# Opening of a hybrid decoder layer: the weight casts are queued behind the cast of h, and the low gate weights ride beside the high ones

## The chip, the core and the metric

The kernel runs on one core of a Trainium2 chip. The metric is the device time of one execution in microseconds. A kernel's time is the median of its runs; beside that there is one profiled execution, from which all rows below come. The engines are called as the profile calls them: PE (TensorE, matrix products), PEld (its weight loads), DVE (VectorE), ACT (ScalarE), POOL (GpSimd) and SP (SyncE, which here only issues transfers).

## What is computed

The reference is one decoder layer over 512 tokens of width 2048, in 32-bit floats. The opening, with which this case deals, computes `h` and the first columns of `h @ w_in`:

```
mod = jax.nn.silu(c) @ w_ada + b_ada
shift, scale, gate = jnp.split(mod[:, None, :], 3, axis=-1)
h = rms_norm(x, norm_w) * (1.0 + scale) + shift
proj = h @ w_in
aq, ak, av, ag, d_qkv, dz, db, da, mg_a, mg_b = jnp.split(proj, _split_points(), axis=-1)
...
beta = jax.nn.sigmoid(db.astype(f32))
g = -jnp.exp(a_log) * jax.nn.softplus(da.astype(f32) + dt_bias)
```

The rest (sliding-window attention, the gated delta rule, the merge and the output product) is the same in both kernels.

## The kernel before

Each product of 32-bit operands is made of three products of a shorter format. An operand is split into a high part, the cast of the value, and a low part, the value less the high part. `mm3` then adds up high weights times high `h`, high weights times low `h`, and low weights times high `h`. `split` makes the two parts: the cast on ACT (line 61, tile `whi`), the subtraction on DVE (line 62, tile `wlo`). For `h` the two parts are `hh` (ACT, line 476) and `hl` (DVE, line 480).

`startup` is the opening. The width of 2048 is cut into 16 blocks of 128 rows, numbered `kt` from 0 to 15. For each block the kernel needs the shift and the scale of these 128 rows. They are sums of `silu(c)` over two tiles of `w_ada` of 1 MB each (tile `wa`, lines 394 and 458). In blocks with an even number, and in block 15, one of the two sums is made on PE (line 449, picked up on line 455), the other on DVE; in the other blocks both are made on DVE. In block 0 both are made on PE. From the sums ACT makes the shift and scale (lines 468 and 471, tile `sh`), then `h` of the block (line 475), then `hh`; DVE makes `hl`. With these `products` runs 21 products of 512 columns: seven column groups of weights (two for `v`, one of 64 columns called `ba` for the gates' `db` and `da`, four for `k`), three products each.

The weights of these column groups come as one tile of 832 KB for two blocks (tile `raw`, line 215, source `w_st`). `split_half` splits the half that belongs to one block, 832 columns. `whl` keeps three pairs of high and low tiles, `wraw` two raw tiles, `st2` seven `wa` tiles. `half_done` puts the next split on a list, and `weight_tick` runs the list at the end of a block.

The order in which the instructions stand on each engine is made by a scheduler from the program; each engine then works through its own row in order. `behind(a, b)` tells the scheduler that `a` must stand after `b`. `split_behind` is used for this in the opening: the subtraction of the weights of block `kt + 1` is put behind the last DVE sum of `wa` for that block (`last_sum`). The cast of these weights has no such rule in the kernel before. `made["h"]` holds the latest cast of `h`; when the split of the weights of block `kt + 1` is put out, it is the cast of `h` of that same block.

After the opening, `gates` takes the 64 rows of `ba`, turns them with four transposes (line 566) and makes the gates of them.

Of the kernel before, what the change touches and what calls it, by code (L numbers as in the profile page):

```python
# [7 lines left out]
F32 = mybir.dt.float32  # L8
# [3 lines left out]
ALU = mybir.AluOpType  # L12
# [4 lines left out]
P = 128  # L17
T = 512
D = 2048
KT = D // P  # L20
NTB = T // P
EPS = 1e-6
KH = 16
VH = 32
# [7 lines left out]
NST = 4  # L32
# [13 lines left out]
class Layer:  # L46
# [174 lines left out]
    def split_half(self):  # L221
        n = self.half_split
        j = n // 2
        if j < len(self.jobs):
            w = self.jobs[j][1].shape[-1] // 2
            raw = self.raws[j]
            hi = self.whl.tile([P, 1024], F32R, tag="whi", name="whi")
            lo = self.whl.tile([P, 1024], F32R, tag="wlo", name="wlo")
            h, l = self.split(hi[:, :w], lo[:, :w], raw[:, (n % 2) * w : (n % 2 + 1) * w])
            if self.split_behind:  # L230
                self.behind(l, self.split_behind)
            self.halves[n] = (hi, lo)
            self.half_split += 1
            if n % 2:
                del self.raws[j]
                self.due.append(self.load_job)
# [144 lines left out]
    def startup(self, st):  # L381


        tc, nc, a, const = self.tc, self.nc, self.a, self.const
# [3 lines left out]
        acc, loads, sums, made = {}, {}, {}, {}  # L388
        last_sum = {}

        def load_ada(kt):
# [13 lines left out]
            out=row, in0=scb[0:1, :], scalar=1.0, in1=row, op0=ALU.add, op1=ALU.mult  # L405
# [23 lines left out]
        for g in range(4):  # L429
# [3 lines left out]
            out=bn, in0=self.b_ada[:, KT : 2 * KT], scalar=1.0, in1=self.norm_w, op0=ALU.add, op1=ALU.mult  # L433
# [52 lines left out]
        n = 0  # L486
        for q in range(4):
            ps = self.psc.tile([P, T], F32, tag="sc", name="rowb")
# [5 lines left out]
        for b2 in (0, 2):  # L494
# [3 lines left out]
            for b in (b2, b2 + 1):  # L498
                xt, u = xts[b], b % 2
                nc.vector.tensor_scalar(out=xt, in0=xt, scalar1=r[:, u : u + 1], scalar2=None, op0=ALU.mult)  # L500
                for q in range(4):
                    i = n % 6
                    ps = pa.tile([P, 4, P], F32, tag=f"x{i}", name="xtp") if i < 2 else self.psc.tile([P, 4, P], F32, tag="sc", name="xtp")
# [11 lines left out]
        def products(kt, parts):  # L515
            f, l = kt == 0, kt == KT - 1
            wh, wl = parts
            x = (self.hh[:, kt, :], self.hl[:, kt, :])
            for ps, o, n in outs:
                self.mm3(ps, (wh[:, o : o + n], wl[:, o : o + n]), x, f, l)  # L520

        low(0, adaln(0))
        ada_sums(1)
        acc_v = [pa.tile([P, T], F32, tag=f"x{i}", name=f"v{i}") for i in range(2)]
        acc_ba = self.pmm.tile([P, T], F32, tag="mm", name="ba")[: 2 * VH]
        self.acc_k = [self.psc.tile([P, T], F32, tag="sc", name=f"k{n}") for n in range(NST)]
        outs = [(acc_v[0], 0, P), (acc_v[1], P, P), (acc_ba, 2 * P, 2 * VH)]
        outs += [(self.acc_k[n], 320 + n * P, P) for n in range(NST)]
        for kt in range(KT):
            nxt = kt + 1 < KT and adaln(kt + 1)  # L530
            if kt + 3 < KT:
                load_ada(kt + 3)
            if kt + 2 < KT:
                ada_sums(kt + 2)
            if kt + 1 < KT:
                low(kt + 1, nxt)
            products(kt, self.half(f"st{kt // 2}"))
            self.half_done()
            self.split_behind = last_sum.get(kt + 1)
            self.weight_tick()  # L540
        self.split_behind = None
        self.ba = self.dnc.tile([2 * VH, T], F32, name="ba")
        nc.vector.tensor_copy(out=self.ba, in_=acc_ba)
        for i in range(2):
            vt = s2.tile([P, T], F32, tag="h32", name="vt")
# [5 lines left out]
    def gates(self, sp):  # L551

        nc, a, dnc = self.nc, self.a, self.dnc
        pt = self.ptp
        bd = sp.tile([P, NTB, 2 * VH], F32, name="bd")
        S = [P, NTB, VH]
        self.sums = sp.tile([P, 4, P], F32, name="sums")
        nc.sync.dma_start(out=self.sums, in_=a["k_sums"])
        al = sp.tile([P, VH], F32, name="al")
        nc.sync.dma_start(out=al, in_=a["a_log"].partition_broadcast(P))  # L560
        dtb = sp.tile([P, VH], F32, name="dtb")
        nc.sync.dma_start(out=dtb, in_=a["dt_bias"].partition_broadcast(P))
        nc.scalar.activation(al, al, AF.Exp)
        pb = pt.tile([P, NTB, 2 * VH], F32, tag="tp", name="pb")
        for c in range(NTB):
            nc.tensor.transpose(pb[:, c, :], self.ba[:, c * P : (c + 1) * P], self.ident[: 2 * VH, : 2 * VH])
        nc.vector.tensor_copy(out=bd, in_=pb)
        beta = self.beta = dnc.tile(S, F32, name="beta")
        e = sp.tile(S, F32, name="ge")
        nc.scalar.activation(e, bd[:, :, 0:VH], AF.Exp, scale=-1.0)  # L570
        nc.vector.tensor_scalar(out=e, in0=e, scalar1=1.0, scalar2=None, op0=ALU.add)
        nc.vector.reciprocal(out=beta, in_=e)
        y = sp.tile(S, F32, name="gy")
        nc.vector.tensor_tensor(out=y, in0=bd[:, :, VH : 2 * VH], in1=dtb.unsqueeze(1).to_broadcast(S), op=ALU.add)
        u = sp.tile(S, F32, name="gu")
        nc.vector.scalar_tensor_tensor(out=u, in0=y, scalar=-1.0, in1=y, op0=ALU.mult, op1=ALU.min)
        nc.scalar.activation(u, u, AF.Exp)
        w = sp.tile(S, F32, name="gw")
        nc.vector.tensor_scalar(out=w, in0=u, scalar1=1.0, scalar2=None, op0=ALU.add)
        lw = sp.tile(S, F32, name="glw")  # L580
        nc.scalar.activation(lw, w, AF.Ln)
        d = sp.tile(S, F32, name="gd")
        nc.vector.scalar_tensor_tensor(out=d, in0=w, scalar=-1.0, in1=u, op0=ALU.add, op1=ALU.subtract)
        nc.vector.reciprocal(out=w, in_=w)
        nc.vector.tensor_tensor(out=d, in0=d, in1=w, op=ALU.mult)
        nc.vector.tensor_tensor(out=lw, in0=lw, in1=d, op=ALU.subtract)
        nc.vector.scalar_tensor_tensor(out=y, in0=y, scalar=0.0, in1=lw, op0=ALU.max, op1=ALU.add)
        nc.vector.scalar_tensor_tensor(
            out=y, in0=y, scalar=-1.0, in1=al.unsqueeze(1).to_broadcast(S), op0=ALU.mult, op1=ALU.mult
        )  # L590
        fl = lambda t: t.rearrange("p c h -> p (c h)")
        yield 8
        pg = pt.tile([P, 4, P], F32, tag="tp", name="pg")
        for n in range(4):
            nc.tensor.matmul(pg[:, n, :], lhsT=self.sums[:, n, :], rhs=fl(y), start=True, stop=True)
        G = sp.tile(S, F32, name="G")
        nc.vector.tensor_copy(out=fl(G), in_=pg[:, 0, :])
        EG = sp.tile(S, F32, name="EG")
        nc.scalar.activation(fl(EG), pg[:, 1, :], AF.Exp)
        self.kd = dnc.tile(S, F32, name="kd")  # L600
        nc.scalar.activation(fl(self.kd), pg[:, 2, :], AF.Exp)
        self.egl = dnc.tile(S, F32, name="egl")
        nc.scalar.activation(fl(self.egl), pg[:, 3, :], AF.Exp)
        self.neg_eg = dnc.tile(S, F32, name="neg_eg")
        nc.vector.tensor_scalar(out=self.neg_eg, in0=EG, scalar1=-1.0, scalar2=None, op0=ALU.mult)
        self.neg_g = dnc.tile(S, F32, name="neg_g")
        nc.vector.tensor_scalar(out=self.neg_g, in0=G, scalar1=-1.0, scalar2=None, op0=ALU.mult)
        self.neg_beta = dnc.tile(S, F32, name="neg_beta")
        nc.vector.tensor_scalar(out=self.neg_beta, in0=beta, scalar1=-1.0, scalar2=None, op0=ALU.mult)
        self.g_rows = self.dram.tile([VH, T], F32, name="g_rows")  # L610
        self.eg_rows = self.dram.tile([VH, T], F32, name="eg_rows")
        self.b_rows = self.dram.tile([VH, T], F32, name="b_rows")
        for src, dst in ((G, self.g_rows), (EG, self.eg_rows), (beta, self.b_rows)):
            yield 1
            pr = pt.tile([VH, T], F32, tag="tp", name="pr")
            for c in range(NTB):
                nc.tensor.transpose(pr[:, c * P : (c + 1) * P], src[:, c, :], self.ident)
            rows = sp.tile([VH, T], F32, tag="rows", name="rows", bufs=2)
            nc.vector.tensor_copy(out=rows, in_=pr)
            nc.sync.dma_start(out=dst, in_=rows)  # L620
        self.dump("G", G)
        self.dump("beta", beta)
# [1063 lines left out]
def layout(i):  # L1686
# [3 lines left out]
    f = lambda x: np.ascontiguousarray(x)  # L1690
    w_in, w_ada = i["w_in"][0], i["w_ada"][0]
    o = {}
# [9 lines left out]
    o["b_ada"] = f(i["b_ada"][0].reshape(48, P).T)  # L1702
    o["b_gate"] = f(i["b_ada"][0].reshape(3, D)[2])
    o["norm_w"] = f(i["norm_w"][0].reshape(KT, P).T)
    st = np.concatenate([w_in[:, 2304:2560], w_in[:, 16896:16960], w_in[:, 6656 : 6656 + NST * P]], 1)
    o["w_st"] = f(st.reshape(KT // 2, 2, P, STW).transpose(0, 2, 1, 3).reshape(KT // 2, P, 2 * STW))
    ch = lambda w: w.reshape(KT, P, -1, P).transpose(2, 1, 0, 3).reshape(-1, P, KT * P)
    o["w_ch"] = f(np.concatenate([ch(w_in[:, 4608:16896]), ch(w_in[:, 19008:]), ch(w_in[:, :2304]), ch(w_in[:, 2560:4608]), ch(w_in[:, 16960:19008])]))
# [57 lines left out]
```

## Time and profile before

| | before |
|---|---|
| median of 3 runs | 2849.0 us (2845.32 to 2851.39) |
| time of the profiled execution | 2842.31 us |
| its span, first to last instruction | 2840.5 us |
| granted TensorE clock over the span | 0.999 |
| PE busy in the span | 2812.2 us (99%) |
| DVE, ACT busy | 1940.2 us (68%), 1195.2 us (42%) |
| products of blocks 0 to 15 in the opening | from 31.08 us to 124.86 us |

In the rows of a timeline the first number is the start in us, the second the busy time in us, then come engine, line, operation, output and inputs; the brackets tell how long the engine was idle before, and what ended that. A row of the windows gives for a stretch the busy time of each engine with the count of its instructions, then the granted PE clock, the share of the transfer engines that was busy, and GB/s. Consecutive starts on an engine are closer than the durations, since instructions overlap a little; the sums below go from start to start.

### The profile page before, as it was taken

To read this page: it belongs to the slowest core of one execution; us is meant where nothing else is said; L and a number is where in the kernel's file an instruction comes from. 1 tells how busy PE (TensorE), PEld (TensorE's weight loads), DVE (VectorE), ACT (ScalarE), POOL (GpSimd) and SP (SyncE) were. 2 spreads that over 40 slices of the span, in tenths; PEclk is the share of its full clock that TensorE was granted. 3 is DMA by queue.
4 is the path that set the end of the run, shared out by engine and by line. 5 is a ranking of instruction groups with operands and counts; after the bars stand their busy time and mean duration, and the time that the engine had idled before them with its cause. 6 is when DMAs were issued, how large, how long until landed. Compare 5 with 4: busy or idle time off the path is not lost.

```text
span 2840.5 us, 38583 instructions
## 1 busy us (share of the span) xinstructions
PE 2812.2 (99%) x14312; PEld 2305.0 (81%) x14312; DVE 1940.2 (68%) x3142; ACT 1195.2 (42%) x2452; POOL 146.9 (5%) x124
## 2 busy tenths in 40 slices
PE   8999999999999999999999999999999999999999
PEld 5788888887787888888888888888888888888887
DVE  7866776867757666778766666666656766664676
ACT  5555443244454343433434333333334554432443
POOL 0010100100000010000001000000000000000000
PEclk9999999999999999999999999999999999999999
DMA  9878764322244253366777666666646887885684
GB/s 404 333 230 238 255 223 143 110 91 92 80 118 137 87 167 105 116 209 218 243 259 262 231 223 241 230 231 235 242 167 233 300 311 246 303 276 179 245 312 172
DMA packets 228368, 603.30 MB, mean 212 GB/s; under 512 B 76210, under 2 KB 102450, under 8 KB 187858
## 3 DMA queue, kind: packets, MB, share of 16 engines
q1 hardware_dynamic: 228180, 600.83, 62.2%
q8 instruction: 113, 1.85, 0.3%
q14 instruction: 75, 0.61, 0.1%
HBM read 480.35 MB, written 118.17 MB: 211 GB/s over the span
## 4 chain that ended last, share of the span: by engine, by line
PE 94%; DVE 2%; DMA 2%; ACT 1%; issue 1%; SPq 0%; POOL 0%; DVEq 0%; ACTq 0%; POOLq 0%
PE mm L259 22%; PE mm L261 21%; PE mm L260 21%; PE m L260 5%; PE m L259 5%; PE m L261 5%; PE S L1416 1%; PE pv L960 1%; PE O L1474 1%; PE pod L979 1%; PE pod L978 1%; PE pod L975 1%; PE pp L950 1%; DMA E<-g_rows 1%; PE k L259 1%; PE k L260 1%
## 5 line engine op out<-in xcount | busy, mean ns | idle before, releaser
L259 PE MATMUL mm<-hh,whi 128*128 128x512 f32 x2784 | 1129.1, 406 | 0.0
L261 PE MATMUL mm<-hh,wlo 128*128 128x512 f32 x2784 | 1089.2, 391 | 0.0
L260 PE MATMUL mm<-hl,whi 128*128 128x512 f32 x2784 | 1086.4, 390 | 0.0
L62 DVE TENSOR_TENSOR wlo<-raw,whi 128x1024 fp32r<-128x1024 f32 (+1 forms) x532 | 653.2, 1228 | 438.1 <-ACT whi L61 432.4
L61 ACT CAST whi<-raw 128x1024 fp32r<-128x1024 f32 (+1 forms) x532 | 555.9, 1045 | 838.3 <-PE mm L260 595.5
L261 PEld LDWEIGHTS mm<-hh,wlo 128*128 128x128 f32 x2784 | 522.5, 188 | 113.8 <-issue 0.4
L259 PEld LDWEIGHTS mm<-hh,whi 128*128 128x128 f32 x2784 | 523.4, 188 | 111.7 <-issue 10.6
L260 PEld LDWEIGHTS mm<-hl,whi 128*128 128x128 f32 x2784 | 524.0, 188 | 100.8 <-issue 1.6
L1225 DVE TENSOR_TENSOR q<-q,q 128x1024 f32<-128x1024 f32 x96 | 124.8, 1300 | 0.7 <-issue 0.6
L773 ACT ACTIVATE E<-E,neg_g 128x128 f32<-128x128 f32 x256 | 80.9, 394 | 90.5 <-POOL E L767 78.9
L810 DVE TENSOR_TENSOR A<-A,atmp 128x62 f32<-128x62 f32 (+30 forms) x124 | 109.2, 881 | 0.4
L802 DVE TENSOR_TENSOR atmp<-A 128x62 f32<-128x62 f32 (+30 forms) x124 | 107.4, 866 | 0.3
L907 POOL TENSOR_TENSOR qe<-qe,yq 128x512 f32<-128x512 f32 x32 | 55.6, 1755 | 920.1 <-DMA qe<-eg_rows 532.2
L980 ACT COPY osb<-pod 128x256 f32<-128x256 f32 x64 | 23.8, 372 | 152.6 <-PE pod L979 152.6
L767 POOL TENSOR_SCALAR_AFFINE_SELECT E<-E 128x512 f32<-128x512 f32 x64 | 59.3, 941 | 433.2 <-DMA E<-g_rows 241.5
L962 ACT COPY vn<-pv 128x256 f32<-128x256 f32 x64 | 23.8, 372 | 124.4 <-PE pv L960 124.4
L631 DVE SCALAR_TENSOR_TENSOR yv<-mm,convh,yv 128x511 f32<-128x511 f32 (+2 forms) x96 | 71.2, 742 | 1.1
L967 DVE TENSOR_SCALAR vs<-vn,kd 128x128 f32<-128x128 f32 x96 | 23.1, 283 | 58.3 <-ACT vn L962 58.3
L1444 ACT ACTIVATE sm<-sm,mx,rs 128x128 f32<-128x128 f32 x128 | 61.5, 482 | 3.0 <-DVE mx L1439 3.0
L990 DVE SCALAR_TENSOR_TENSOR S<-S,egl,pod 128x128 f32<-128x128 f32 x64 | 19.2, 342 | 51.0 <-ACT junk L983 51.0
L636 ACT ACTIVATE th<-yv 128x512 f32<-128x512 f32 x32 | 20.2, 631 | 76.3 <-DVE yv L631 73.7
L458 DVE SCALAR_TENSOR_TENSOR wa<-wa,silu_cb 128x2048 f32<-128x2048 f32 x22 | 50.1, 2283 | 0.0
(438 smaller groups left out, 3661.4 us busy)
## 6 DMA issues: line engine op xcount, KB each, us to landing
raw<-in_w_ch SPq DMA_DIRECT2D x158, 1024.0 KB
wa<-in_w_ada_ss SPq DMA_DIRECT2D x32, 1024.0 KB
q<-in_w_od SPq DMA_DIRECT2D x64, 512.0 KB
g_d<-q SPq DMA_DIRECT2D x64, 512.0 KB
raw<-g_d SPq DMA_DIRECT2D x32, 1024.0 KB
raw<-in_w_od SPq DMA_DIRECT2D x24, 1024.0 KB
gw<-in_w_ada_gate SPq DMA_DIRECT2D x16, 1024.0 KB
E<-g_rows SPq DMA_DIRECT2D x64, 256.0 KB
```

What stands on the lines that cost most here:

```text
L61: h = self.nc.scalar.copy(out=hi, in_=src)
L62: l = self.nc.vector.tensor_tensor(out=lo, in0=src, in1=hi.bitcast(F32), op=ALU.subtract)
L259: nc.tensor.matmul(ps, lhsT=wh, rhs=xh, start=first, stop=False)
L260: nc.tensor.matmul(ps, lhsT=wh, rhs=xl, start=False, stop=False)
L261: self.last_mm = nc.tensor.matmul(ps, lhsT=wl, rhs=xh, start=False, stop=last)
L631: nc.vector.scalar_tensor_tensor(out=y[:, s:], in0=ps[:, : T - s], scalar=w[:, j : j + 1], in1=y[:, s:], op0=ALU.mult, op1=ALU.add)
L767: self.last_mask = self.nc.gpsimd.affine_select(out=E, in_=E, pattern=[[0, NTB], [1, P]], compare_op=ALU.is_ge, fill=NEG, base=0, channel_ ...
L773: self.nc.scalar.activation(E[:, c, :], E[:, c, :], AF.Exp, bias=self.neg_g[:, c, h : h + 1])
L802: eng.tensor_tensor(out=t, in0=A[:, m : m + 1, m + 1 :].to_broadcast([P, m, n]), in1=A[:, :m, m : m + 1].to_broadcast([P, m, n]), op=ALU.mult,
L810: self.behind(eng.tensor_tensor(out=A[:, :m, m + 1 :], in0=A[:, :m, m + 1 :], in1=t, op=ALU.add))
L1225: self.behind(nc.vector.tensor_tensor(out=q[f], in0=q[x], in1=q[y], op=ALU.add))
L1444: nc.scalar.activation(t, t, AF.Exp, scale=r[:, h : h + 1], bias=mx[:, h : h + 1], accum_out=den[:, h : h + 1])
```

## The change

There are two edits, both in the opening.

The first edit is in `split_half`. `split_behind` is now a pair. The cast of the weights (now line 231) is put behind the cast of `h` of the same block, `made["h"]`. The subtraction stays behind the last DVE sum.

The second edit concerns the 64 gate columns. They move to the end of the 832 columns. Their low part is no longer written into `wlo` but into `whi`, right behind the high part, so that high and low stand side by side in 128 columns. One product of these 128 columns with `hh` then takes the place of two of 64 columns. High times high lands in rows 0 to 63 of `ba`, low times high in rows 64 to 127; the product with `hl` is still of 64 columns. A block has 20 products instead of 21. The subtraction of one half becomes two instructions (both line 232): 768 columns into `wlo` and 64 into `whi`. In `gates` the four transposes take 128 rows, and one more addition joins the two halves.

```diff
             hi = self.whl.tile([P, 1024], F32R, tag="whi", name="whi")
             lo = self.whl.tile([P, 1024], F32R, tag="wlo", name="wlo")
-            h, l = self.split(hi[:, :w], lo[:, :w], raw[:, (n % 2) * w : (n % 2 + 1) * w])
+            src = raw[:, (n % 2) * w : (n % 2 + 1) * w]
+            if w < 1024:
+                h = self.nc.scalar.copy(out=hi[:, :w], in_=src)
+                sub = lambda out, s: self.nc.vector.tensor_tensor(
+                    out=out, in0=src[:, s], in1=hi[:, s].bitcast(F32), op=ALU.subtract
+                )
+                wide, ba = slice(0, 6 * P), slice(6 * P, w)
+                l = sub(lo[:, wide], wide)
+                low = (l, sub(hi[:, w : w + 2 * VH], ba))
+            else:
+                h, l = self.split(hi[:, :w], lo[:, :w], src)
+                low = (l,)
             if self.split_behind:
-                self.behind(l, self.split_behind)
+                self.behind(h, self.split_behind[0])
+                for i in low if self.split_behind[1] else ():
+                    self.behind(i, self.split_behind[1])
...
-            for ps, o, n in outs:
+            for i, (ps, o, n) in enumerate(outs):
+                if i == 2:
+                    pair = [(P, x[0]), (2 * VH, x[1])]
+                    for m, xm in pair[::-1] if l else pair:
+                        nc.tensor.matmul(
+                            acc_ba[:m], lhsT=wh[:, 6 * P : 6 * P + m], rhs=xm, start=f and m == P, stop=l and m == P
+                        )
                 self.mm3(ps, (wh[:, o : o + n], wl[:, o : o + n]), x, f, l)
...
-        outs = [(acc_v[0], 0, P), (acc_v[1], P, P), (acc_ba, 2 * P, 2 * VH)]
-        outs += [(self.acc_k[n], 320 + n * P, P) for n in range(NST)]
+        outs = [(acc_v[0], 0, P), (acc_v[1], P, P)]
+        outs += [(self.acc_k[n], 2 * P + n * P, P) for n in range(NST)]
...
-            self.split_behind = last_sum.get(kt + 1)
+            self.split_behind = (made["h"], last_sum.get(kt + 1))
...
-        self.ba = self.dnc.tile([2 * VH, T], F32, name="ba")
+        self.ba = self.dnc.tile([P, T], F32, name="ba")
...
-        pb = pt.tile([P, NTB, 2 * VH], F32, tag="tp", name="pb")
+        pb = pt.tile([P, NTB, P], F32, tag="tp", name="pb")
         for c in range(NTB):
-            nc.tensor.transpose(pb[:, c, :], self.ba[:, c * P : (c + 1) * P], self.ident[: 2 * VH, : 2 * VH])
-        nc.vector.tensor_copy(out=bd, in_=pb)
+            nc.tensor.transpose(pb[:, c, :], self.ba[:, c * P : (c + 1) * P], self.ident)
+        nc.vector.tensor_copy(out=bd, in_=pb[:, :, 0 : 2 * VH])
+        nc.vector.tensor_tensor(out=bd, in0=pb[:, :, 2 * VH :], in1=bd, op=ALU.add)
```

What the edits do to the order is seen best on ACT, from the shift and scale of block 4 to the cast of `h` of block 5. `whi_554` and `whi_611` are the high weights of blocks 4 and 5, `h32_520` and `h32_561` their `h` (one number higher after the change), `acc` the sums of DVE. Before:

```order
L471 ACTIVATE sh_517<-acc_470,bn_154,norm_wT_114 128x1
L61 CAST whi_554<-raw_454 128x832
L475 ACTIVATE h32_520<-xnT_94,sh_517 128x512
L61 CAST whi_611<-raw_454 128x832
L476 CAST hh_76<-h32_520 128x512
L468 ACTIVATE sh_558<-acc_527,b_adaT_112 128x1
L471 ACTIVATE sh_558<-acc_527,bn_154,norm_wT_114 128x1
L475 ACTIVATE h32_561<-xnT_94,sh_558 128x512
L476 CAST hh_76<-h32_561 128x512
```

The same stretch of ACT's row after the change:

```order
L484 ACTIVATE sh_518<-acc_471,bn_154,norm_wT_114 128x1
L488 ACTIVATE h32_521<-xnT_94,sh_518 128x512
L489 CAST hh_76<-h32_521 128x512
L231 CAST whi_554<-raw_454 128x832
L481 ACTIVATE sh_559<-acc_528,b_adaT_112 128x1
L484 ACTIVATE sh_559<-acc_528,bn_154,norm_wT_114 128x1
L488 ACTIVATE h32_562<-xnT_94,sh_559 128x512
L489 CAST hh_76<-h32_562 128x512
L231 CAST whi_611<-raw_454 128x832
```

Both casts stood ahead of the `hh` of block 4; now each stands right behind the `hh` of its own block, and `whi_611` has moved past the four instructions of block 5.

On DVE, the stretch from the sum of block 4 to the first sum of block 7 stands so before:

```order
L458 SCALAR_TENSOR_TENSOR wa_427,acc_470<-wa_427,silu_cb_93 128x2048
L62 TENSOR_TENSOR wlo_555<-raw_454,whi_554 128x832
L458 SCALAR_TENSOR_TENSOR wa_466,acc_527<-wa_466,silu_cb_93 128x2048
L480 TENSOR_TENSOR hl_77<-h32_520,hh_76 128x512
L458 SCALAR_TENSOR_TENSOR wa_468,acc_527<-wa_468,silu_cb_93 128x2048
L62 TENSOR_TENSOR wlo_612<-raw_454,whi_611 128x832
L458 SCALAR_TENSOR_TENSOR wa_525,acc_568<-wa_525,silu_cb_93 128x2048
L480 TENSOR_TENSOR hl_77<-h32_561,hh_76 128x512
L62 TENSOR_TENSOR wlo_653<-raw_552,whi_652 128x832
L458 SCALAR_TENSOR_TENSOR wa_564,acc_625<-wa_564,silu_cb_93 128x2048
```

DVE after the change, from the same sum on:

```order
L471 SCALAR_TENSOR_TENSOR wa_428,acc_471<-wa_428,silu_cb_93 128x2048
L232 TENSOR_TENSOR wlo_555<-raw_454,whi_554 128x768
L471 SCALAR_TENSOR_TENSOR wa_467,acc_528<-wa_467,silu_cb_93 128x2048
L493 TENSOR_TENSOR hl_77<-h32_521,hh_76 128x512
L232 TENSOR_TENSOR whi_554<-raw_454,whi_554 128x64
L471 SCALAR_TENSOR_TENSOR wa_469,acc_528<-wa_469,silu_cb_93 128x2048
L232 TENSOR_TENSOR wlo_612<-raw_454,whi_611 128x768
L232 TENSOR_TENSOR whi_611<-raw_454,whi_611 128x64
L471 SCALAR_TENSOR_TENSOR wa_526,acc_569<-wa_526,silu_cb_93 128x2048
L493 TENSOR_TENSOR hl_77<-h32_562,hh_76 128x512
L232 TENSOR_TENSOR wlo_653<-raw_552,whi_652 128x768
L471 SCALAR_TENSOR_TENSOR wa_565,acc_626<-wa_565,silu_cb_93 128x2048
```

Sums and subtractions keep their places; the 64-column subtractions are new, one behind the wide one in an odd block, one behind `hl` in an even block.

On PE, block 14 after the change begins so; the transposed sum of block 15 (line 462) stands ahead of it:

```order
L462 MATMUL ada<-wa,silu_cr 32x128 x16
L272 MATMUL v_351<-hh,whi 128x512
L272 MATMUL v_352<-hh,whi 128x512
L468 MATMUL ada<-pick,adas 128x1
L536 MATMUL ba<-hh,whi 128x512
L272 MATMUL k_354<-hh,whi 128x512
L272 MATMUL k_355<-hh,whi 128x512
L272 MATMUL k_356<-hh,whi 128x512
L272 MATMUL k_357<-hh,whi 128x512
L273 MATMUL v_351<-hl,whi 128x512
L274 MATMUL v_351<-hh,wlo 128x512
```

And before:

```order
L449 MATMUL ada<-wa,silu_cr 32x128 x16
L261 MATMUL k_357<-hh,wlo 128x512
L259 MATMUL v_351<-hh,whi 128x512
L455 MATMUL ada<-pick,adas 128x1
L259 MATMUL v_352<-hh,whi 128x512
L259 MATMUL ba<-hh,whi 64x512
L259 MATMUL k_354<-hh,whi 128x512
L259 MATMUL k_355<-hh,whi 128x512
L259 MATMUL k_356<-hh,whi 128x512
L259 MATMUL k_357<-hh,whi 128x512
L260 MATMUL v_351<-hl,whi 128x512
```

In both, the seven products that need only `hh` and `whi` come first, and the products with `hl` and `wlo` after them; the product of the gate columns with `hh` now has 128 rows of output.

More of the change, by code (lines that the diff above doesn't have):

```diff
@@ L524, in startup @@
         acc_v = [pa.tile([P, T], F32, tag=f"x{i}", name=f"v{i}") for i in range(2)]
-        acc_ba = self.pmm.tile([P, T], F32, tag="mm", name="ba")[: 2 * VH]
+        acc_ba = self.pmm.tile([P, T], F32, tag="mm", name="ba")
         self.acc_k = [self.psc.tile([P, T], F32, tag="sc", name=f"k{n}") for n in range(NST)]
-        outs = [(acc_v[0], 0, P), (acc_v[1], P, P), (acc_ba, 2 * P, 2 * VH)]
-        outs += [(self.acc_k[n], 320 + n * P, P) for n in range(NST)]
+        outs = [(acc_v[0], 0, P), (acc_v[1], P, P)]
+        outs += [(self.acc_k[n], 2 * P + n * P, P) for n in range(NST)]
         for kt in range(KT):
@@ L1704, in layout @@
     o["norm_w"] = f(i["norm_w"][0].reshape(KT, P).T)
-    st = np.concatenate([w_in[:, 2304:2560], w_in[:, 16896:16960], w_in[:, 6656 : 6656 + NST * P]], 1)
+    st = np.concatenate([w_in[:, 2304:2560], w_in[:, 6656 : 6656 + NST * P], w_in[:, 16896:16960]], 1)
     o["w_st"] = f(st.reshape(KT // 2, 2, P, STW).transpose(0, 2, 1, 3).reshape(KT // 2, P, 2 * STW))
```

## The prediction

> **What bounds the opening now.** I read the page first, then the windows of the opening, then the timeline of PE, DVE and ACT there.
>
> ```profile
> PE 2812.2 (99%) x14312; PEld 2305.0 (81%) x14312; DVE 1940.2 (68%) x3142; ACT 1195.2 (42%) x2452; POOL 146.9 (5%) x124
> 97.50:108.50 11.00, 11.00 (x88) 8.45 (x76) 9.78 (x11) 5.72 (x11) 0.00 (x0) 1.00 1.01 420
> ```
>
> PE is busy 99% of the span, so nothing outside the opening can give back much of what the opening loses. In the window PE is full, DVE is busy 9.78 of 11 us, and the transfers run at 420 GB/s. PE sets the pace, but DVE is only 1.2 us behind it.
>
> ```profile
> 53.14 0.73 PE L259 MATMUL v<-hh,whi 128*128 128x512 f32 x2
> ...
> 97.68 0.73 PE L259 MATMUL v<-hh,whi 128*128 128x512 f32 x2
> ...
> 108.70 0.73 PE L259 MATMUL v<-hh,whi 128*128 128x512 f32 x2
> ...
> 120.06 0.39 PE L259 MATMUL v<-hh,whi 128*128 128x512 f32 x1
> ...
> 124.86 0.39 PE L259 MATMUL mm<-hh,whi 128*128 128x512 f32 x1
> ```
>
> These are the first products of blocks 3, 11, 13 and 15, and the first after the opening. Two blocks take 108.70 - 97.68 = 11.02 us. The 21 products of block 15 take 4.80 us, 0.2286 each. So 42 products are 9.60 us of the pair's 11.02, and 1.42 us go to the sum on PE.
>
> DVE and ACT in such a pair:
>
> ```profile
> 88.89 1.02 DVE L62 TENSOR_TENSOR wlo<-raw,whi 128x832 fp32r<-128x832 f32 x1 [1.22 <-ACT whi L61]
> 89.83 2.28 DVE L458 SCALAR_TENSOR_TENSOR wa<-wa,silu_cb 128x2048 f32<-128x2048 f32 x1
> ...
> 92.04 0.69 DVE L480 TENSOR_TENSOR hl<-h,hh 128x512 fp32r<-128x512 f32 x1
> 92.64 2.28 DVE L458 SCALAR_TENSOR_TENSOR wa<-wa,silu_cb 128x2048 f32<-128x2048 f32 x1
> ...
> 94.86 1.02 DVE L62 TENSOR_TENSOR wlo<-raw,whi 128x832 fp32r<-128x832 f32 x1
> 95.79 2.28 DVE L458 SCALAR_TENSOR_TENSOR wa<-wa,silu_cb 128x2048 f32<-128x2048 f32 x1
> ```
>
> ```profile
> 87.98 0.87 ACT L61 CAST whi<-raw 128x832 fp32r<-128x832 f32 x1
> 88.76 0.81 ACT L475 ACTIVATE h<-xnT,sh 128x512 f32<-128x512 f32 x1
> 89.48 0.87 ACT L61 CAST whi<-raw 128x832 fp32r<-128x832 f32 x1
> 90.25 0.62 ACT L476 CAST hh<-h 128x512 fp32r<-128x512 f32 x1
> ...
> 94.97 0.39 ACT L471 ACTIVATE sh<-acc,bn,norm_wT 128x1 f32<-128x1 f32 x1 [2.52 <-DVE wa L458]
> 95.39 0.82 ACT L475 ACTIVATE h<-xnT,sh 128x512 f32<-128x512 f32 x1
> 96.24 0.62 ACT L476 CAST hh<-h 128x512 fp32r<-128x512 f32 x1
> ```
>
> One of the two `wlo` of a pair, at 88.89, waits 1.22 us for its cast; the other, at 94.86, starts at once, because its cast was done at 89.48, before the sums ahead of it.
>
> **The first edit, on the steady pairs.** After the change every `wlo` stands on DVE right behind the last sum of its own block (in even blocks `hl` of the block before stands between), while its cast stands on ACT behind that block's `sh`, `h` and `hh`, which need this very sum. So from the start of the last sum to the start of `wlo` there is one chain: sum to `sh` 94.97 - 92.64 = 2.33; `sh` to `h` 0.42; `h` to `hh` 0.85; `hh` to the next ACT instruction 0.53; the cast 0.87; cast's end to `wlo` 88.89 - 88.85 = 0.04. The 0.53 is from these rows:
>
> ```profile
> 39.59 0.62 ACT L476 CAST hh<-h 128x512 fp32r<-128x512 f32 x1
> 40.12 0.26 ACT L454 COPY adas<-ada 128x128 f32<-128x128 f32 x1
> ```
>
> The chain is 5.04 us. DVE has nothing else to do in it beyond the sum (2.21 from start to start) and, in even blocks, `hl` (0.60): what is behind `wlo` in its row, the next block's sums, waits too, and with them ACT and PE.
>
> From start to start on DVE: `wlo` of 832 columns 89.83 - 88.89 = 0.94, of 768 columns 0.94 x 768/832 = 0.87 (an estimate by width). No row has a subtraction of 64 columns. The nearest small ones are these:
>
> ```profile
> 142.05 0.22 DVE L605 TENSOR_SCALAR neg_eg<-EG 128x128 f32<-128x128 f32 x1
> 142.18 0.22 DVE L607 TENSOR_SCALAR neg_g<-G 128x128 f32<-128x128 f32 x1
> ```
>
> They are 0.13 apart and 0.22 long, which are my bounds; I take 0.14, since 64 columns are fewer than 128 and read two inputs.
>
> - From `wlo` of an odd block to `wlo` of the even one: 0.87 + 0.14 + 5.04 = 6.05 us.
> - From there to the next odd one: 0.87 + a first sum 2.21 + `hl` 0.60 + 0.14 + 5.04 = 8.86 us.
> - A pair: 14.91 us, where PE alone took 11.02. That is 3.89 us more per pair, and DVE becomes the bound, by waiting 2.83 + 2.23 = 5.06 us per pair instead of 1.22.
>
> **The start.** Here the edit gains.
>
> ```profile
> 27.64 0.89 ACT L61 CAST whi<-raw 128x832 fp32r<-128x832 f32 x1
> ...
> 28.90 0.84 ACT L475 ACTIVATE h<-xnT,sh 128x512 f32<-128x512 f32 x1
> ...
> 30.39 0.63 ACT L476 CAST hh<-h 128x512 fp32r<-128x512 f32 x1
> ...
> 37.35 0.89 ACT L61 CAST whi<-raw 128x832 fp32r<-128x832 f32 x1 [5.55 <-PE k L260]
> ```
>
> ```profile
> 33.87 2.29 DVE L458 SCALAR_TENSOR_TENSOR wa<-wa,silu_cb 128x2048 f32<-128x2048 f32 x1
> 40.26 0.51 PE L259 MATMUL v<-hh,whi 128*128 128x512 f32 x1 [1.71 <-ACT hh L476]
> ```
>
> A cast between `h` and `hh` of block 0 goes away: `hh` starts at 28.90 + 0.85 = 29.75 instead of 30.39, 0.64 sooner. The cast at 37.35 waited for a tile that PE held until the end of block 0, and block 1's `sh` stood behind it; that wait goes. So the last sum of block 1 starts at 33.87 - 0.64 = 33.23, and its `wlo` and PE's block 1 at 33.23 + 5.04 = 38.27 instead of 40.26: 2.0 us gained. Block 2: 38.27 + 6.05 = 44.32. Its `hl` starts 0.82 before that (0.04 + 0.87 + 0.53, less 0.62 for `hh`) at 43.50; then `hl` 0.60, a sum 2.21, `wlo` 0.87 lead to 47.18, and the chain of 5.04 to `wlo` of block 3 at 52.22, against 53.14 for PE's block 3 before. What is gained is 0.9 us.
>
> **The rest.** Five pairs lead to block 13 at 52.22 + 74.55 = 126.77, then 14 at 132.82 and 15 at 138.87 (both with one DVE sum, 6.05 each). In block 14 PE does the seven `hh` products and waits for `hl`, which stands behind the sum of block 15: 132.82 + 0.87 + 0.14 + 2.21 + 0.69 = 136.73. From there PE has 13 + 20 products without a wait: 33 x 0.2286 = 7.54, ending at 144.27. Before, it was 124.86. The opening gets 19.4 us longer.
>
> **The second edit.** It removes 16 products, 16 x 0.2286 = 3.66 us of PE. PE waits for DVE in every pair (14.91 against 40 x 0.2286 + 1.42 = 10.56), so I count 0 for it, besides the one product already left out in block 14 and in block 15. It would count in full only with PE as the bound. The 16 small subtractions are in the chain above, 0.14 each.
>
> ```profile
> 126.31 0.46 PE L566 MATMUL pb<-ident,ba 64*128 64x64 f32 x4
> 127.53 0.42 DVE L567 COPY bd<-pb 128x256 f32<-128x256 f32 x1
> ```
>
> In `gates` the transposes may take up to twice their 0.46 us on PE and the addition costs another 0.42 on DVE; between 0 and 0.9 us, and I take 0, since the gates had until 134 us to wait for other loads. The weight load of 128 columns instead of 64 hides beside the product, as for `v` and `k`.
>
> **Loads** do not become the bound.
>
> ```profile
> wa<-in_w_ada_ss SPq DMA_DIRECT2D x32, 1024.0 KB
> raw<-in_w_st SPq DMA_DIRECT2D x8, 832.0 KB
> ```
>
> A pair needs four `wa` and one `raw`, 4928 KB or 5.05 MB, 12.0 us at 420 GB/s. SP issues a `raw` only when the odd block's subtraction has read the old one, and the `wa` loads queue behind it; at 14.91 us a pair there are 2.9 us to spare.
>
> **Sum.** 2842.3 + 19.4 = 2861.7 us for the profiled execution, which was 6.7 us under the median of the runs. Against the median, 2849.0 + 19.4 = 2868.4.
>
> **Rivals.**
>
> *PE goes cold in its new idle stretches, and the loss is larger.* Each pair has about 3.3 us of waits inside its blocks (some 1.9 for `hl` in the odd, 1.4 in the even).
>
> ```profile
> 37.50:40.90 3.40, 1.68 (x36) 1.32 (x35) 0.66 (x2) 2.81 (x6) 0.00 (x0) 1.00 1.01 424
> 40.90:44.30 3.40, 3.31 (x8) 2.31 (x9) 3.40 (x6) 1.35 (x3) 0.00 (x0) 0.50 1.00 417
> 208.20:211.60 3.40, 1.57 (x11) 1.49 (x12) 2.94 (x11) 2.73 (x7) 0.00 (x0) 1.00 0.23 81
> 211.60:215.00 3.40, 3.40 (x19) 2.81 (x18) 1.77 (x3) 1.52 (x6) 0.00 (x0) 1.00 0.82 163
> ```
>
> Once 3.4 us with PE busy for 1.68 were followed by a window at half clock, once with 1.57 they were not. A cold window costs 1.7 us of PE work. Two per pair with all waits kept give 10.56 + 3.4 + 3.3 = 17.3 us, 2.4 over DVE's 14.91; over six pairs 14 us more, 2883. Against it: a late PE finds `hl` ready and has no idle stretch left, so the loss grows only up to the waits. It decides when a pair of PE passes 14.91. [...]
>
> *DVE does not hold PE up, and the edits pay.* It would need the casts early enough that each `wlo` waits no more than the present 1.22 us per pair. Then PE stays the bound, with 3.66 us of products less and the 2.0 us at block 1: 2849.0 - 5.7 = 2843.3, on the edge of what can be told from no change (0.2%, 5.7 us, is about what the measurement tells). For it speaks only the gain at the start; against it, that the sum, `sh`, `h`, `hh`, cast and `wlo` depend on each other in this order. It decides where the chain shrinks from 5.04 to about 3.1 us.
>
> *The order does less than it says*, because some `wlo` finds its cast done, as at 94.86 now. If this held for one block of each pair, 2.83 us of the wait would go: 14.91 - 2.83 = 12.08, 1.06 over 11.02. Six pairs make 6.4, less the 0.9 gained at the start 5.5, so 2849.0 + 5.5 = 2854.5. The row on ACT gives no block such a cast.
>
> **Chances.** 0.80 for the forecast, 0.09 for the cold PE, 0.05 for edits that pay, 0.06 for the partial case. The forecast's own range: small subtractions at 0.22 add 1.2 us, `gates` up to 0.9, one cold window in blocks 14 and 15 1.7; hand-overs 0.05 off in each of 15 blocks 0.8 either way; the median of the runs moves some 3 us. That is 2862 to 2876. For eight in ten I give 2860 to 2878. Faster by over 0.2%: 0.02; within 0.2%: 0.08 (half of the partial case with it); slower: 0.90.
>
> **What would show it.** After the change, each `wlo` on DVE waits for ACT's `whi`: about 2.8 us in odd and 2.2 us in even blocks, over 30 us in all. Wide subtractions two blocks apart are 14.9 us apart. PE's block 1 starts near 38.3, block 15 near 139, the first product after the opening near 144. PE has idle stretches with `hl` and `whi` as releasers, DVE busy falls to two thirds in a pair's window, and the transfers fall under 420 GB/s. From 150 us on both kernels should run alike, shifted. The forecast is wrong if `wlo` finds its cast done, or if the granted clock is 0.50 in many windows of the opening.

## The result and the profile after

The changed kernel takes 2870.98 us (median of 4 runs, 2865.76 to 2874.23) against 2847.16 us before (4 runs, 2843.12 to 2851.39): a ratio of 1.0081 with an interval of 1.0066 to 1.0095, slower by 24 us. Its profiled execution took 2874.23 us with a span of 2872.5 us. All rows of "the changed kernel" below are of this execution.

From its page, the engines' busy time and the chain that ended last:

```profile
PE 2818.7 (98%) x14296; PEld 2308.0 (80%) x14296; DVE 1939.4 (68%) x3159; ACT 1196.4 (42%) x2452; POOL 148.4 (5%) x124
...
PE 88%; DVE 5%; DMA 3%; ACT 3%; issue 1%; SPq 0%; POOL 0%; DVEq 0%; ACTq 0%; POOLq 0%
```

And the chain on the page of the kernel before:

```profile
PE 94%; DVE 2%; DMA 2%; ACT 1%; issue 1%; SPq 0%; POOL 0%; DVEq 0%; ACTq 0%; POOLq 0%
```

The 16 products are gone from PE (14296 against 14312), yet PE's share of the chain has fallen by 6 points, and DVE and ACT have taken over most of it. The view by windows says where. This is one pair of blocks of the changed kernel, from the wide subtraction of block 9 to that of block 11:

```profile
97.67:112.57 14.90, 11.21 (x74) 8.26 (x74) 10.02 (x12) 5.93 (x12) 0.00 (x0) 1.00 0.84 340
```

Before, a pair took 11.02 us with PE full. Now PE is busy 11.21 of 14.90 us, DVE 10.02 and ACT 5.93, and the transfers have fallen from 420 to 340 GB/s. No engine and no queue is full, which is what a chain of hand-overs looks like. The timeline of DVE in the pair before it, and of ACT at its end:

```profile
82.76 0.96 DVE L232 TENSOR_TENSOR wlo<-raw,whi 128x768 fp32r<-128x768 f32 x1 [2.74 <-ACT whi L231]
83.63 0.22 DVE L232 TENSOR_TENSOR whi<-raw,whi 128x64 fp32r<-128x64 f32 x1
83.77 2.29 DVE L471 SCALAR_TENSOR_TENSOR wa<-wa,silu_cb 128x2048 f32<-128x2048 f32 x1
...
88.81 0.96 DVE L232 TENSOR_TENSOR wlo<-raw,whi 128x768 fp32r<-128x768 f32 x1 [2.14 <-ACT whi L231]
89.69 2.28 DVE L471 SCALAR_TENSOR_TENSOR wa<-wa,silu_cb 128x2048 f32<-128x2048 f32 x1
...
91.90 0.69 DVE L493 TENSOR_TENSOR hl<-h,hh 128x512 fp32r<-128x512 f32 x1
92.50 0.22 DVE L232 TENSOR_TENSOR whi<-raw,whi 128x64 fp32r<-128x64 f32 x1
92.64 2.28 DVE L471 SCALAR_TENSOR_TENSOR wa<-wa,silu_cb 128x2048 f32<-128x2048 f32 x1
...
97.67 0.96 DVE L232 TENSOR_TENSOR wlo<-raw,whi 128x768 fp32r<-128x768 f32 x1 [2.74 <-ACT whi L231]
```

```profile
94.97 0.39 ACT L484 ACTIVATE sh<-acc,bn,norm_wT 128x1 f32<-128x1 f32 x1 [2.65 <-DVE wa L471]
95.38 0.82 ACT L488 ACTIVATE h<-xnT,sh 128x512 f32<-128x512 f32 x1
96.23 0.62 ACT L489 CAST hh<-h 128x512 fp32r<-128x512 f32 x1
96.76 0.88 ACT L231 CAST whi<-raw 128x832 fp32r<-128x832 f32 x1
```

Read the two together from 92.64: DVE starts the last sum of block 9. ACT can make `sh` only at 94.97, then `h`, `hh`, and at 96.76 the cast, now the last of the four. `wlo` starts at 97.67 after 2.74 us in which DVE had nothing to do, and the sums of the next block stand behind it. The other block of the pair waits 2.14 us. On PE this comes out as gaps before the products that need `whi` or `hl`:

```profile
38.98 0.50 PE L272 MATMUL v<-hh,whi 128*128 128x512 f32 x1 [0.38 <-ACT whi L231]
...
86.72 0.49 PE L273 MATMUL v<-hl,whi 128*128 128x512 f32 x1 [1.83 <-DVE hl L493]
...
97.69 0.50 PE L272 MATMUL v<-hh,whi 128*128 128x512 f32 x1 [0.55 <-ACT whi L231]
...
145.12 0.39 PE L272 MATMUL mm<-hh,whi 128*128 128x512 f32 x1
```

The last of these rows is the first product after the opening, at 145.12 us against 124.86. The waits of 25 to 150 us, by who waited for whom (us in total, times, longest):

```profile
ACT sh L484 <- DVE wa L471: 33.6, 14, 2.8
DVE wlo L232 <- ACT whi L231: 27.1, 11, 2.7
...
PE v L273 <- DVE hl L493: 14.0, 9, 2.2
...
PE v L272 <- ACT whi L231: 5.0, 8, 1.0
```

ACT waits for DVE, DVE for ACT, and PE for both.

### The profile page after: what moved, and what is told of

It reads as the page before. It is cut to its first block, busy times and chain, and to the rows that moved or that the text cites. A ratio compares the mean times of both kernels' runs of the same rounds, so it can differ in the third digit from the quotient of the medians.

```text
span 2872.5 us, 38576 instructions
## 1 busy us (share of the span) xinstructions
PE 2818.7 (98%) x14296; PEld 2308.0 (80%) x14296; DVE 1939.4 (68%) x3159; ACT 1196.4 (42%) x2452; POOL 148.4 (5%) x124
## 4 chain that ended last, share of the span: by engine, by line
PE 88%; DVE 5%; DMA 3%; ACT 3%; issue 1%; SPq 0%; POOL 0%; DVEq 0%; ACTq 0%; POOLq 0%
PE mm L272 21%; PE mm L274 21%; PE mm L273 21%; PE m L273 5%; PE m L272 5%; PE m L274 5%; DVE wa L471 2%; PE S L1436 1%; DMA E<-g_rows 1%; PE pv L980 1%; PE O L1494 1%; PE pod L999 1%; DVE wlo L62 1%; PE pod L998 1%; PE pod L995 1%
## 5 line engine op out<-in xcount | busy, mean ns | idle before, releaser
L62 DVE TENSOR_TENSOR wlo<-raw,whi 128x1024 fp32r<-128x1024 f32 x516 | 636.3, 1234 | 433.1 <-ACT whi L61 425.2
L61 ACT CAST whi<-raw 128x1024 fp32r<-128x1024 f32 x516 | 541.5, 1050 | 829.3 <-PE mm L273 589.8
L1000 ACT COPY osb<-pod 128x256 f32<-128x256 f32 x64 | 23.8, 372 | 152.6 <-PE pod L999 152.6
L982 ACT COPY vn<-pv 128x256 f32<-128x256 f32 x64 | 23.8, 372 | 124.5 <-PE pv L980 124.5
L1010 DVE SCALAR_TENSOR_TENSOR S<-S,egl,pod 128x128 f32<-128x128 f32 x64 | 19.3, 343 | 51.0 <-ACT junk L1003 51.0
```

Of the source, the lines that this page charges most:

```text
L61: h = self.nc.scalar.copy(out=hi, in_=src)
L62: l = self.nc.vector.tensor_tensor(out=lo, in0=src, in1=hi.bitcast(F32), op=ALU.subtract)
```

## The experiments

Theory A is the prediction's: DVE, which works through its row in order, waits behind the chain from sum to cast. B says that part of the loss lies past 150 us, C that the second edit costs something by itself, D that a late cast starves PE directly, without DVE. The six experiments are set against the kernel before on the same chip: 2845.87 us (median of 23 runs) for the first four, 2845.27 us (15 runs) for the last two. The row of the changed kernel's first measurement is the comparison with 2847.16 us given above. The times of pairs and of the first product are from each kernel's profiled execution, the medians and ratios from all its runs.

| kernel | us per pair | first product after the opening | median | ratio (interval) |
|---|---|---|---|---|
| before | 11.02 | 124.86 | | 1 |
| changed, the first measurement | 14.91 | 145.12 | 2870.98 | 1.0081 (1.0066 to 1.0095) |
| changed, again | 14.91 | 144.13 | 2868.06 | 1.008 (1.0068 to 1.0092) |
| second edit alone | 10.57 | 123.79 | 2846.79 | 1.0002 (0.9994 to 1.0011) |
| first edit alone | 14.77 | 144.38 | 2865.58 | 1.0067 (1.0054 to 1.008) |
| cast one block earlier | 10.57 | 122.00 | 2843.45 | 0.9996 (0.9987 to 1.0005) |
| subtraction later | 11.88 | 123.57 | 2847.67 | 1.0009 (1.0000 to 1.0018) |
| cast ahead of `hh` | 13.57 | 135.91 | 2859.51 | 1.005 (1.0036 to 1.0064) |

**The changed kernel again.** No edit. The profiled execution of the changed kernel was 32.0 us longer than that of before, of which the opening explains 20.3.

> The changed kernel once more, with more rounds. Theory A (DVE waits in its own order for casts that depend on its last sum; some 19.5 us, all of it in the opening) expects the first product after the opening 19 to 20.5 us later than before and a ratio near 1.007. Theory B (the rest of the profiled execution's difference, some 11 us after 150 us, belongs to the change too) expects the same loss after 150 us again and a ratio of 1.009 to 1.011.

The opening ended at 144.13, and the whole span was 2864.9 us, 7.6 less than in the first execution, with only 1.0 of that in the opening. From the first product on it took 2720.8 us, against 2727.4 in the first execution and 2715.6 in the one of before. So 6.6 of the 11.7 us that the first seemed to lose past the opening were its own, and theory B falls as far as those go; 5.1 us are left. The ratio, 1.008, lies between what A and B expected, and its interval reaches into both, so that the total does not decide between them.

**The second edit alone.** In the changed kernel:

```
-                self.behind(h, self.split_behind[0])
```

> Only the second edit: the gate columns in one 128-column product, casts free as before. Theory A: no wait for the cast chain comes in; DVE needs 9.86 us a pair plus the wait of even blocks (0.7 to 1.2), so pairs take 10.6 to 11.1 us against 11.02 and the time is 0 to 3 us under before (ratio 0.999 to 1.000). Theory C (the second edit itself costs, by its small subtractions or its longer gates) expects 2 to 5 us over before (1.001 to 1.002).

The casts stand again where they stood before. Two of the wide subtractions, and two waits of DVE from 25 to 150 us:

```profile
66.85 0.96 DVE L232 TENSOR_TENSOR wlo<-raw,whi 128x768 fp32r<-128x768 f32 x1 [0.63 <-ACT whi L231]
...
77.42 0.96 DVE L232 TENSOR_TENSOR wlo<-raw,whi 128x768 fp32r<-128x768 f32 x1 [0.63 <-ACT whi L231]
```

```profile
DVE wlo L232 <- ACT whi L231: 4.4, 6, 1.2
...
DVE wa L470 <- DMA wa<-in_w_ada_ss: 2.8, 2, 2.3
```

A pair takes 10.57 us, 0.45 less than before: two products less, 2 x 0.2286. Both kernels had block 6 at 66.85 us, so this holds for three pairs, 1.35 us; in the next one DVE waits for a load of `wa`, and the first product came 1.1 us sooner. The total is the same: the interval reaches from 1.7 us less to 3.1 us more. The gain of 0 to 3 us that theory A expected is not shown either. So the second edit by itself has next to nothing of the 22 us, and a cost of 2 to 3 us, theory C's lower end, is neither shown nor excluded.

**The first edit alone**, made in the kernel before:

```
-                self.behind(l, self.split_behind)
+                self.behind(h, self.split_behind[0])
+                if self.split_behind[1]:
+                    self.behind(l, self.split_behind[1])
...
-            self.split_behind = last_sum.get(kt + 1)
+            self.split_behind = (made["h"], last_sum.get(kt + 1))
```

> Only the first edit: each cast behind the cast of h of its block, 21 products of the old columns. Theory A: the same chain of 5.04 us with one subtraction of 0.94 instead of 0.87 and 0.14, so a pair takes 14.8 us, and block 15 ends 18 to 19.5 us later than before; ratio 1.006 to 1.008. Theory C expects most of the loss to be gone: ratio under 1.004.

DVE's timeline, the subtractions of three blocks in a row:

```profile
67.03 1.02 DVE L62 TENSOR_TENSOR wlo<-raw,whi 128x832 fp32r<-128x832 f32 x1 [2.74 <-ACT whi L61]
...
73.01 1.03 DVE L62 TENSOR_TENSOR wlo<-raw,whi 128x832 fp32r<-128x832 f32 x1 [2.14 <-ACT whi L61]
...
81.80 1.02 DVE L62 TENSOR_TENSOR wlo<-raw,whi 128x832 fp32r<-128x832 f32 x1 [2.74 <-ACT whi L61]
```

81.80 - 67.03 = 14.77 us per pair, with the same two waits as in the changed kernel. One line about the order of ACT's row gives the loss: 1.0067, and the first product at 144.38, 19.5 us after that of before.

**The cast one block earlier**, with both edits:

```
+            held = made["h"]
             nxt = kt + 1 < KT and adaln(kt + 1)
...
-            self.split_behind = (made["h"], last_sum.get(kt + 1))
+            self.split_behind = (held, last_sum.get(kt + 1))
```

The cast of block `kt + 1` now stands behind the `hh` of block `kt`; the rule is still there, but ahead of the sums of its own block.

> Both edits, but the cast of the weights of block kt+1 stands behind the cast of h of block kt, one block sooner. Theory A: each cast is done before its subtraction comes up in odd blocks, even blocks wait under 1.3 us; a pair takes 10.6 to 11.1 us, the early gain at block 1 (about 2 us) stays, and the time is 2 to 5 us under before (ratio 0.998 to 0.9995). If the place of the cast behind any h were what costs (theory D: ACT itself is late), the loss would stay above 5 us.

The subtractions of two even blocks, and DVE's waits from 90 to 125 us:

```profile
74.83 0.96 DVE L232 TENSOR_TENSOR wlo<-raw,whi 128x768 fp32r<-128x768 f32 x1 [0.62 <-ACT whi L231]
...
85.40 0.96 DVE L232 TENSOR_TENSOR wlo<-raw,whi 128x768 fp32r<-128x768 f32 x1 [0.63 <-ACT whi L231]
```

```profile
DVE wa L471 <- DMA wa<-in_w_ada_ss: 3.6, 2, 2.3
DVE wlo L232 <- ACT whi L231: 1.3, 2, 0.6
```

All of the loss is gone: 10.57 us a pair, and a first product at 122.00. That is 22 to 23 us sooner than in the two executions of the changed kernel, by moving a cast by one block. Against the kernel before it is 2.9 us in the trace; the total, 0.9996, just misses the 0.998 to 0.9995 expected and cannot be told from no change. Toward the end the pairs no longer wait for ACT but for the loads of `wa`, 3.6 us in the list. The transfers ran at 423 GB/s from 40 to 100 us; at that rate the 5.05 MB of a pair take 11.9 us, longer than the pair's 10.57, so that by the author's estimate what was loaded ahead is used up.

**The subtraction later**, cast as in the changed kernel:

```
-            self.split_behind = (made["h"], last_sum.get(kt + 1))
+            self.split_behind = (made["h"], sums.get(kt + 2) or last_sum.get(kt + 1))
```

Here the late cast stays, and only DVE's row changes: the subtraction goes behind the first DVE sum of the block after.

> Both edits, the casts stay late (behind the cast of h of their own block), but the subtraction is put behind the first DVE sum of the block after, so that DVE makes a sum while ACT runs through sh, h, hh and the cast. Theory A (what costs is DVE standing still in its order, with sums queued behind the wait) expects no wait of DVE for whi over 0.5 us, a pair of 10.6 us by PE until the loads limit it, the first product after the opening at 120 to 123 us, and a time 1 to 4 us under before (ratio 0.9985 to 0.9997). Theory D (the late cast itself starves PE, which needs whi at the head of every block) expects pairs over 12 us still and a ratio over 1.002.

```profile
81.96 2.29 DVE L471 SCALAR_TENSOR_TENSOR wa<-wa,silu_cb 128x2048 f32<-128x2048 f32 x1 [1.34 <-DMA wa<-in_w_ada_ss]
...
84.78 0.95 DVE L232 TENSOR_TENSOR wlo<-raw,whi 128x768 fp32r<-128x768 f32 x1
...
96.66 0.95 DVE L232 TENSOR_TENSOR wlo<-raw,whi 128x768 fp32r<-128x768 f32 x1
```

```profile
DVE wa L471 <- DMA wa<-in_w_ada_ss: 8.9, 8, 3.1
...
PE v L272 <- ACT whi L231: 3.2, 5, 0.8
```

The subtractions have no bracket: no wait of DVE for the cast is left, though the cast is as late as in the changed kernel. PE still waits for the late cast, 3.2 us in all from 25 to 150 us, but its 14.0 us of waits for `hl` are down to 0.6. So theory D falls as the cause of the loss; what cost the time was DVE standing still behind the cast with the next sums in its row. A small part may still be the late cast's own: the first product came 1.6 us later than with the cast one block earlier. The pair now takes 96.66 - 84.78 = 11.88 us, and what ends DVE's waits is the load of `wa`. The first product, at 123.57, and the ratio, 1.0009, came out above what theory A expected (120 to 123 us, 0.9985 to 0.9997), but below theory D's 1.002; the opening was 1.3 us shorter than before, and the excess lies behind it.

**The cast ahead of `hh`**, behind `h`:

```
-            nc.scalar.activation(h32, xnT[:, kt, :], AF.Identity, scale=sh[:, 1:2], bias=sh[:, 0:1])
+            made["a"] = nc.scalar.activation(h32, xnT[:, kt, :], AF.Identity, scale=sh[:, 1:2], bias=sh[:, 0:1])
...
-            self.split_behind = (made["h"], last_sum.get(kt + 1))
+            self.split_behind = (made["a"], last_sum.get(kt + 1))
```

This cuts one link out of the chain and leaves the rest.

> Both edits, but each cast stands between h and hh of its block instead of behind hh. Theory A: the chain from the last sum to the subtraction shrinks by 0.85 + 0.53 - 0.72 = 0.66 us to 4.38, a pair to 13.59 us, and the opening by some 15 x 0.66 = 9.9 us against the changed kernel: first product after it near 134.5 us, ratio 1.003 to 1.0045. If the wait were not this chain (theory D: PE's own need for hh and whi, which both still come 4.9 us after the sum), a pair would stay near 14.9 us and the ratio near 1.007.

```profile
77.55 0.96 DVE L232 TENSOR_TENSOR wlo<-raw,whi 128x768 fp32r<-128x768 f32 x1 [2.08 <-ACT whi L231]
...
82.93 0.96 DVE L232 TENSOR_TENSOR wlo<-raw,whi 128x768 fp32r<-128x768 f32 x1 [1.48 <-ACT whi L231]
...
91.12 0.96 DVE L232 TENSOR_TENSOR wlo<-raw,whi 128x768 fp32r<-128x768 f32 x1 [2.08 <-ACT whi L231]
```

Each wait is 0.66 us shorter (2.74 to 2.08, 2.14 to 1.48), and a pair takes 13.57 us against 13.59 expected. The loss per pair follows the length of the chain, as far as this one link shows it. The end of the opening, 135.91, was 1.4 us later than expected, and the ratio, 1.005, is over the 1.003 to 1.0045 expected. PE now waits at the start of blocks for `hh`, 6.9 us in all, but that did not slow the pairs. The reason for the 1.4 us stands in PE's rows. The last product that waited was, in the changed kernel and in this one:

```profile
131.44 0.50 PE L273 MATMUL v<-hl,whi 128*128 128x512 f32 x1 [1.83 <-DVE hl L493]
```

```profile
122.24 0.50 PE L273 MATMUL v<-hl,whi 128*128 128x512 f32 x1 [1.31 <-DVE hl L493]
```

In both it is the wait for the `hl` of block 13. From there PE runs to the first product after the opening without a wait, 13.68 us in the changed kernel and 13.67 here. So only the chains of 13 blocks count and not of 15, as the expectation had it: 13 x 0.66 = 8.6 us instead of 9.9, which is 1.3 of the 1.4 us.

## Why the prediction was right, point by point

- **The chain.** 97.67 - 92.64 = 5.03 us against 5.04; from odd to even 6.05 and from even to odd 8.86, both as forecast; the pair 14.91 to the hundredth. The rows of before had each link, and only their order was new. (In its reading of before, the prediction calls the cast of 89.48 done at that time. It started then and ended at 90.35, still ahead of the sum at 92.64 and of its subtraction at 94.86.) The three experiments that shorten the chain, put the cast ahead of it, or put the subtraction behind the next sum show that it is the cause.
- **The small subtraction.** 83.77 - 83.63 = 0.14 us, the value taken.
- **The start.** PE began block 1 at 38.98, against 38.27. The first cast of this execution stood at 28.33, where it was 27.64 before; less this 0.69 it is 38.29. In the second execution it was 38.00, with that cast at 27.35.
- **The end.** The last wide subtraction stood at 139.58 (138.87 forecast), the first product at 145.12 (144.27); less the 0.69, each is within 0.2 us. In the second execution it was 144.13: 19.3 us after that of before, 19.4 forecast. The path there was not the forecast one. PE was to wait in block 14 for `hl`, which was there at 136.75 + 0.69 = 137.44, but the row that needs it has no wait:

```profile
137.58 0.41 PE L273 MATMUL v<-hl,whi 128*128 128x512 f32 x1
```

PE's last wait was the one at 131.44, for the `hl` of block 13, and from there it had 53 products and one sum to do (53 x 0.2286 + 1.42 = 13.54 us; it took 13.68). The two paths end within 0.2 us of each other, so that this step of the prediction has its number right by luck; in the experiment with the cast ahead of `hh` the two differ.

- **Loads** did not become the bound in the changed kernel, as forecast (340 GB/s). They do as soon as the chain is gone: the 12.0 us a pair worked out for them showed as 11.88 in the kernel with the later subtraction, where the transfers ran at 424 GB/s from 60 to 100 us. SP's waits for the subtraction ahead of a `raw`, from 25 to 150 us in the kernel before:

```profile
SPq L215 <- DVE wlo L62: 38.0, 9, 9.2
```

- **The waits in all** were 27.1 us in the list, not "over 30": its 11 waits are those of blocks 4 to 14. In blocks 1 to 3 and 15 `hl` stands on DVE ahead of the subtraction and waits for `hh` instead, 1.96 + 1.69 + 1.82 + 1.35 = 6.82 us; with these it is 33.9 us. The subtraction of block 15 is again 6.05 us behind the one before.
- **Cold PE** came about, and cost nothing on the pace. Two windows of the pairs ran at half clock, from 62.91 and from 117.52 (granted clock 0.50 in the rows of the last section); the products that start from 63.35 to 65.91 are 0.43 us apart, those from 66.57 to 67.51, behind that window, 0.23. By these steps such a window costs an estimated 3.41 x (1 - 0.23/0.43) = 1.6 us of PE work, where the prediction has 1.7. From the subtraction of block 3 to that of block 5, and from 11 to 13, in which they fall, it took 14.91 us and 14.90 us, like the other pairs. A late PE found `hl` ready, which was the argument against this rival: in blocks 8 and 10 PE waited 1.30 us for `hl`, in block 12, right after the second cold window, not at all.
- **The second edit at 0** was a little low. `neg_eg` on DVE is among the last instructions that make the gates (142.05 before):

```profile
163.28 0.22 DVE L625 TENSOR_SCALAR neg_eg<-EG 128x128 f32<-128x128 f32 x1
```

From the first product it is 142.05 - 124.86 = 17.19 us before, 163.28 - 145.12 = 18.16 after, 18.28 in the second execution, 17.66 with the first edit alone, 17.68 with the second alone. The first edit alone, with the gates of before, thus has 0.47 us of it, and the second edit's part is 0.5 to 0.6 us rather than 0, within the range of 0 to 0.9. On PE, the product that waits for the gates' `gy` stood still 0.36 us before, and now

```profile
161.28 1.16 PE L615 MATMUL pg<-gy,sums 128*128 128x128 f32 x8 [1.22 <-DVE gy L608]
```

1.22 us; it was 0.84 with the first edit alone and 0.74 with the second alone. The weight load of the gate columns for the product with `hh` took 188 ns for 128 columns, 138 ns for 64 before (medians of 16); the next product starts 0.23 us behind it (142.16 to 142.39), against 0.24 before (103.23 to 103.47), so that the longer load does not show.

- **"From 150 us on both alike."** From `neg_eg` to the end of the span it is 2698.5 us before and 2709.2 and 2702.5 in the two executions of the changed kernel. The other five lie between 2699.9 and 2705.9, and the two ends belong to kernels with the same code there, so single executions differ by some 6 us. The forecast of 2861.7 for a profiled execution stood 12.5 under the first and 5.9 under the second; it was the execution of before that was short, as the prediction had noted.
- **The median** was forecast as 2849.0 + 19.4 = 2868.4, and 2870.98 and 2868.06 came. Part of this closeness is luck: the change was 23.8 and 22.2 us, 4.4 and 2.8 over the 19.4, while the base of 2849.0 lay 1.8 us over the median of four runs and 3.1 over that of 23.

**What stays open.** The trace up to `neg_eg` accounts for 20.4 us in the second execution, the medians differ by 22.2. In four of the five kernels with the second edit the difference of the medians is 1.5 to 3.0 us above what the trace up to `neg_eg` gives, in the fifth 0.3 below, as with the first edit alone. Apart from the one with the later subtraction, what the trace gives is inside each kernel's own interval. So a cost of the second edit past the opening, of up to some 3 us, is neither shown nor excluded.

## What to carry to other kernels

When an instruction is moved on one engine, ask who waits for it on an engine that works through its row in order, as DVE did here, and what stands behind that waiter: the cast itself was 0.87 us and off the path, but DVE's next sums stood behind the subtraction that needs it, and DVE stood still for 2.74 and 2.14 us in each pair. A loop through two engines (sum, shift, `h`, cast, subtraction, next sum) can be worked out from start to start from the rows of a kernel in which the same links are still apart, and it set the pace here with PE at 75%, DVE at 67% and ACT at 40% busy. Either side of the wait can be mended: the producer one block earlier took away the whole loss, the waiter one instruction later all but some 2 us of it, and the next bound, the loads, showed there at 11.88 us a pair, 0.86 over the 11.02 of before.

## What the runs showed of the hardware

In both executions of the changed kernel each half-clock window of the opening lasted 3.41 us (granted clock 0.50, for instance from 62.91 to 66.32), and their starts lay whole multiples of that apart, to within 0.05 us. In the first execution they began at 32.20, 62.90 and 117.50 us: 30.70 and 54.60 apart, which is 9 and 16 steps of 3.41. In the second execution they began at 30.10, 71.05 and 101.75, 12 and 9 such steps apart. Cut in these steps, two of the cold windows of the first execution, each behind the window ahead of it, and one more pair of windows are these (the first number behind the length is PE's busy time, the third from the end the granted clock):

```profile
83.39:86.80 3.41, 1.58 (x7) 0.97 (x7) 3.28 (x5) 0.93 (x3) 0.00 (x0) 1.00 0.57 164
86.80:90.22 3.42, 3.42 (x15) 2.78 (x16) 1.41 (x2) 1.95 (x3) 0.00 (x0) 1.00 1.02 426
114.11:117.52 3.41, 1.56 (x7) 0.96 (x6) 2.37 (x3) 1.54 (x3) 0.00 (x0) 1.00 0.76 267
117.52:120.94 3.42, 3.42 (x9) 2.64 (x8) 2.33 (x2) 1.06 (x2) 0.00 (x0) 0.50 1.00 419
59.50:62.91 3.41, 1.25 (x7) 0.69 (x5) 3.41 (x6) 0.29 (x1) 0.00 (x0) 1.00 1.00 423
62.91:66.32 3.41, 3.41 (x8) 2.58 (x9) 2.20 (x2) 1.15 (x2) 0.00 (x0) 0.50 0.97 392
```

And of the second execution:

```profile
98.37:101.78 3.41, 1.58 (x7) 0.93 (x7) 2.21 (x3) 1.70 (x3) 0.00 (x0) 1.00 0.85 296
101.78:105.19 3.41, 3.41 (x10) 2.63 (x9) 2.47 (x2) 0.91 (x2) 0.00 (x0) 0.50 1.02 430
112.02:115.43 3.41, 1.69 (x9) 1.08 (x7) 3.41 (x5) 0.74 (x3) 0.00 (x0) 1.00 0.48 149
115.43:118.85 3.42, 3.31 (x14) 2.69 (x15) 1.28 (x3) 2.13 (x3) 0.00 (x0) 1.00 1.00 397
```

In these rows, windows with PE busy for 1.25, 1.56 and 1.58 us of 3.41 were followed by one at half clock; one with 1.69 us was not, and at 83.39 one with 1.58 us was not either. The two windows of the prediction do not settle it: there the one with more PE work, 1.68 us, was followed by half clock and the one with 1.57 us was not. So in these rows a busy time near half of a window does not by itself tell what follows, and what does is open. The longest wait of PE in the changed kernel from 25 to 150 us was 2.2 us (the wait for `hl` that ended at 62.81, with the window from 62.91 at half clock).
